# A decoder trunk on one core: modulation loads in three buffers of their own, one more buffer for output weights, row sums made one at a time

## The chip, the cores and the metric

The kernel runs on one core of one Trainium2 chip, as one launch. The metric is the device time of the launch in microseconds (us). Engines are named as in the profile: PE (TensorE, matrix products), DVE (VectorE), ACT (ScalarE), POOL (GpSimd) and SP (SyncE). SP computes nothing: it issues transfers, each in its turn, and POOL issues others.

## The reference

```python
for l in range(DEPTH):                                    # 2 layers
    mod = (silu(c) @ w_ada[l] + b_ada[l]).reshape(B, 9, 1024)
    sh1, sc1, gt1, sh2, sc2, gt2, sh3, sc3, gt3 = ...
    hn = rms_norm(h, g_ffn1[l]) * (1.0 + sc1) + sh1
    h = h + 0.5 * (1.0 + gt1) * swiglu(hn, w_ffn1_in[l], w_ffn1_out[l])
    hn = rms_norm(h, g_mix[l]) * (1.0 + sc2) + sh2
    mixed = concat([attention, rwkv7, short_conv](hn @ w_mix_in[l])) @ w_mix_out[l]
    h = h + (1.0 + gt2) * mixed
    hn = rms_norm(h, g_ffn2[l]) * (1.0 + sc3) + sh3
    h = h + 0.5 * (1.0 + gt3) * swiglu(hn, w_ffn2_in[l], w_ffn2_out[l])
# swiglu(x): gate, up = split(x @ w_in);  (silu(gate) * up) @ w_out,  width 2816
```

The sequence has 512 rows, the model 1024 channels, all in float32. The "modulation" is `mod`: 9 vectors of 1024 numbers a layer, each a product of silu(c) with a 1024 x 1024 matrix.

## The kernel before, in words

The state h is held transposed, in 8 tiles of 128 channels x 512 rows. A float32 product is made of three matmuls (`mm3`, L87 to L89): each factor is split into a high part (ACT casts it, L92, tiles wH, actH, hnH, comH) and a low part (DVE subtracts, L93, tiles wL, actL, hnL, comL), and high x high, high x low and low x high are added in PSUM. So each weight tile that lands from HBM in a raw buffer (`wraw`, two of them, `load_w` L219 and `raw` L288) costs an ACT cast and a DVE subtraction before PE can take it, and the raw buffer is free again when DVE has made wL.

Each layer is ffn1, mix, ffn2. An `ffn` (L263) has 22 columns of 128 hidden units, taken as 11 pairs p:

- The first pairs (four in layer 0's ffn1, two elsewhere) are ordinary products: a projector tile for gate and one for up per column, 24 matmuls of 128 x 512 each, then SiLU and product (L390 to L393).
- Meanwhile `combine(k)`, k = 0 to 3, makes sums and differences of the normed rows (two x, four parts of q, then the split comH and comL, L307 to L315) that the other pairs need. The scratch q lies in a buffer "first" or "crep" by turns.
- The other pairs go through `pair_in` (L332), a Strassen scheme of seven products of 24 matmuls of 128 x 256. Their weights are sums of weight blocks. S is loaded by SP (tag "chain", two buffers), and a second block is added to it by an accumulating transfer that POOL issues (`plus`, L293). Then come a11 (tag "first"), a12 (`wraw`), S3 (tag "third", load and accumulate again), and the last block (`wraw`). ACT copies PSUM results out in between (L342, L346, L351).
- The pairs are cut in two groups, g = 0 with columns 0 to 11 and g = 1 with 12 to 21. After each group comes its output product: for each of 8 output tiles i, two pieces of w_out (`pieces`, L375) and 36 or 30 matmuls, then `residual` (L258) adds to h. Between the groups' output tiles stand modulation steps.

A modulation step (`ada_steps`, L157) loads 512 KB on POOL (L164, tile `wada`) and makes one multiply with a sum on DVE (L149) with `crep`, silu(c) in all partitions. Its loads share the buffers "first", "third" and "chain" with the pairs, and `ada_crep` (L151) loads crep through SP and puts SiLU on ACT. In layer 0's ffn1 it does so twice, since combine uses its buffer in between.

A scheduler lists the instructions by the program's order and priorities, and each engine and each issuing queue then goes through its own list strictly in turn. `tc.issue_after` holds an instruction back in that list behind a named one.

The prediction uses letters for places of the span: A, the first Strassen pair of layer 0's ffn1; B, the end of that ffn's output; C, the start of layer 0's ffn2; D and F, the starts of layer 1's ffn1 and ffn2; E, the end of layer 1's ffn1; G, the start of group 1 in layer 0's ffn1.

Of the kernel before, what the change touches and what calls it, by code (L numbers as in the profile page):

```python
# [8 lines left out]
F32 = mybir.dt.float32  # L9
# [6 lines left out]
P = 128  # L16
D = 1024
T = 512
L = 2
KD = D // P  # L20
# [36 lines left out]
def trunk_kernel(ctx, tc, ins, out, layers=L, phases=("ffn1", "mix", "ffn2")):  # L57
    nc = tc.nc
# [4 lines left out]
    wp = ctx.enter_context(tc.tile_pool(name="wp", bufs=3))  # L63
# [87 lines left out]
    def ada_crep(pool):  # L151
        c = pool.tile([P, D], F32, name="crep", tag="crep", bufs=1)
        nc.sync.dma_start(c, ins["crep"])
        act(c, c, AF.Silu)
        return c

    def ada_steps(pool, crep, n, behind=None):  # L157

        with tc.issue_after(behind.ins) if behind else nullcontext():
            for m, (l, i, k) in enumerate(todo[:n]):  # L160
                if (l, i) not in mod:
                    mod[l, i] = const.tile([P, KD], F32, name=f"mod{l}_{i}")
                w = pool.tile([P, D], F32, name="wada", tag=("first", "third", "chain")[m % 3], bufs=1 + m % 3 // 2)
                nc.gpsimd.dma_start(w, ins["wadaT"][l, i, k])  # L164
                ada_dot(mod[l, i][:, k : k + 1], w, crep)
                k0 = k if m == 0 or k == 0 else k0
# [49 lines left out]
        return hn, scale, stats, apply  # L216


    def load_w(src, n=KD):  # L219

        w = wp.tile([P, KD, P], F32, name="wraw", tag="wraw", bufs=2)
        wH = wp.tile([P, KD, P], F32R, name="wH", tag="wH", bufs=4)
        wL = wp.tile([P, KD, P], F32R, name="wL", tag="wL", bufs=4)
        nc.sync.dma_start(w[:, :n], src)
        split(wH[:, :n], wL[:, :n], w[:, :n])
        return wH, wL

# [35 lines left out]
    def ffn(l, w_in, w_pair, w_out, hn, im, ss, need, then, first=None):  # L263
# [6 lines left out]
        with tc.tile_pool(name="act", bufs=1) as ap_:  # L270
# [5 lines left out]
            xs, waiting, done = {}, [], [None]  # L276

            def flush():
                for f in waiting:
                    done[0] = f()  # L280
                waiting.clear()
# [3 lines left out]
                split(*pair, w)  # L285
                return pair

            def raw(src, tag=None, bufs=1):  # L288
                w = (ap_.tile if tag else wp.tile)([P, KD, P], F32, name=tag or "wraw", tag=tag or "wraw", bufs=bufs if tag else 2)
                nc.sync.dma_start(w, src)  # L290
                return w

            def plus(w, src):  # L293
# [9 lines left out]
            def combine(k):  # L303

                x1, x2 = E("x1"), E("x2")
                for x, kk in ((x1, k), (x2, k + 4)):
                    tt(x, hn[kk][0].bitcast(F32), hn[kk][1].bitcast(F32), ALU.add)  # L307
                tag = ("first", "crep")[k % 2]
                q = ap_.tile([P, 4, H2], F32, name="q", tag=tag, bufs=1)
                tt(q[:, 0], x1[:, lo_], x1[:, hi_], ALU.subtract)  # L310
                stt(q[:, 1], x2[:, hi_], -1.0, q[:, 0], ALU.mult, ALU.subtract)
                tt(q[:, 2], x2[:, hi_], x1[:, hi_], ALU.subtract)
                stt(q[:, 3], q[:, 1], -1.0, x2[:, lo_], ALU.mult, ALU.subtract)
                split(*com[k], q)
# [17 lines left out]
            def pair_in(p):  # L332
                A = lambda g, kh: w_pair[l, p, g, kh]
                turns = ("r0", "r1") if p % 2 else ("r1", "r0")
                pD, pF, pG = (psum([P, 2, H2], n, t) for n, t in zip(("ps_d", "ps_f", "ps_g"), ("mm",) + turns))
                X = new_x(p)
                half_ = lambda n: E(n).rearrange("p (i t) -> p i t", i=2)
                S = raw(A(1, 0), "chain", 2)
                plus(S, A(1, 1))
                prod(pF, hl(S), P1, True)  # L340
                up = half_("up")
                nc.scalar.copy(up, pF)  # L342
                a11 = raw(A(0, 0), "first")
# [24 lines left out]
                def rest():  # L368
                    prod(pD, hl(raw(A(1, 1))), T4, False)
                    tt(gate, pD, gate, ALU.mult)  # L370
                    return put(X, lo_, gate)

                waiting.append(rest)

            def pieces(i, j0, j1):  # L375
                n = (j1 - j0) // 2
                for k0 in (j0, j0 + n):
                    yield k0, n, load_w(w_out[l, i, :, k0 : k0 + n], n)

            crep = None  # L380
            if n_first == 4:
                crep = ada_crep(ap_)
            for g, (j0, j1) in enumerate(GROUPS):
                for p in range(j0 // 2, j1 // 2):
                    if p < n_first:
                        X = new_x(p)
                        for j in (2 * p, 2 * p + 1):
                            pg, pu = next(tiles), next(tiles)
                            s = E("silu")
                            act(s, pg, AF.Silu)  # L390
                            stt(s, s, -1.0, pu, ALU.mult, ALU.mult)
# [12 lines left out]
                flush()  # L404
                if todo and not crep:
                    crep = ada_crep(ap_)
# [788 lines left out]
```

## Time and profile before

| | before |
|---|---|
| median of 3 runs | 2047.09 us (2045.33 to 2048.42) |
| the profiled execution | 2047.34 us |
| its span | 2045.6 us |
| mean granted clock of PE | 0.978 |
| PE busy | 1944.5 us |
| DVE busy | 1427.8 us |
| ACT busy | 840.9 us |
| POOL busy | 131.0 us |

The page gives busy time, share of the span and count of instructions. A row of a timeline has the start in the span, the time, the engine, the line, the operation, the tile written and the tiles read; in brackets stand the idle time of the engine ahead of the instruction and what ended it. In the list of waits, a row has who waited for whom, the total in us, how often, and the longest. The granted clock is 1 at full speed; rows of windows have PE's busy time in a stretch and the clock's mean in it.

### The profile page before, as it was taken

How to read it: one execution, taken by the hardware profiler on the slowest of the kernel's cores; microseconds unless marked ns; L12 is line 12 of the kernel's file. 1: busy time of each engine (PE TensorE's matmuls, PEld its weight loads, DVE VectorE, ACT ScalarE, POOL GpSimd, SP SyncE). 2: the span in 40 equal slices, each digit the busy share in tenths (PEclk: the TensorE clock that was granted, in tenths of full speed). 3: DMA queues.
4: the chain of work that ended last, by engine and by line, in shares of the span. 5: the costliest groups of instructions: out<-in, count | busy, mean ns of one | idle time of the engine just before them, and what ended most of it. 6: DMA issues, size and time to landing. Idle time of an engine off the chain costs nothing.

```text
span 2045.6 us, 32890 instructions
## 1 busy us (share of the span) xinstructions
PE 1944.5 (95%) x13428; PEld 1698.5 (83%) x13428; DVE 1427.8 (70%) x2228; ACT 840.9 (41%) x1267; POOL 131.0 (6%) x212
## 2 busy tenths in 40 slices
PE   8969999899999899999988999998999988999999
PEld 7859899786677789899877989987767767998997
DVE  6667687667875777767776776777587667673772
ACT  4433254346322345245244523533553234542551
POOL 0011111100000000110100011110000000010100
PEclk9989999999999899999988999999999998999999
DMA  7566875520122345885654577653202142564643
GB/s 285 199 178 206 274 189 167 193 75 32 53 66 89 83 151 169 278 216 171 204 150 132 171 254 236 186 189 123 83 21 76 51 134 74 164 191 119 188 114 99
DMA packets 104454, 308.72 MB, mean 151 GB/s; under 512 B 23408, under 2 KB 24432, under 8 KB 103280
## 3 DMA queue, kind: packets, MB, share of 16 engines
q1 hardware_dynamic: 76080, 203.86, 29.1%
q0 software_dynamic: 28224, 102.77, 19.6%
q8 instruction: 105, 1.72, 0.3%
q14 instruction: 45, 0.37, 0.1%
HBM read 303.18 MB, written 3.41 MB: 150 GB/s over the span
## 4 chain that ended last, share of the span: by engine, by line
PE 74%; DVE 14%; DMA 6%; ACT 4%; issue 2%; POOL 0%; ACTq 0%; SPq 0%; DVEq 0%; POOLq 0%
PE ps_mm L87 11%; PE ps_mm L88 11%; PE ps_mm L89 11%; PE ps_d L324 6%; PE ps_d L326 6%; PE ps_d L325 6%; PE ps_f L326 3%; PE ps_f L324 3%; PE ps_f L325 3%; DVE wL L93 3%; DMA wraw<-in_w1o 2%; DVE wada L149 2%; PE ps_g L324 2%; PE ps_g L326 2%; PE ps_g L325 2%
## 5 line engine op out<-in xcount | busy, mean ns | idle before, releaser
L92 ACT CAST wH<-wraw 128x1024 fp32r<-128x1024 f32 (+2 forms) x292 | 268.4, 921 | 598.1 <-PE ps_mm L88 193.0
L93 DVE TENSOR_TENSOR wL<-wraw,wH 128x1024 fp32r<-128x1024 f32 (+2 forms) x292 | 308.2, 1058 | 124.4 <-ACT wH L92 122.8
L87 PE MATMUL ps_mm<-hnH,wH 128*128 128x512 f32 (+1 forms) x760 | 281.9, 377 | 36.8 <-ACT hnH L213 30.0
L89 PE MATMUL ps_mm<-hnH,wL 128*128 128x512 f32 (+1 forms) x760 | 282.3, 373 | 17.5 <-DVE wL L93 17.5
L89 PE MATMUL ps_mm<-actH,wL 128*128 128x512 f32 (+1 forms) x744 | 283.6, 381 | 8.6 <-DVE wL L93 8.6
L88 PE MATMUL ps_mm<-hnL,wH 128*128 128x512 f32 (+1 forms) x760 | 285.3, 376 | 0.1
L87 PE MATMUL ps_mm<-actH,wH 128*128 128x512 f32 (+1 forms) x744 | 283.8, 381 | 0.5 <-ACT wH L92 0.3
L88 PE MATMUL ps_mm<-actL,wH 128*128 128x512 f32 (+1 forms) x744 | 283.1, 380 | 0.0
L324 PE MATMUL ps_d<-comH,wH 128*128 128x256 f32 x816 | 227.7, 279 | 0.1
L325 PE MATMUL ps_d<-comL,wH 128*128 128x256 f32 x816 | 225.7, 277 | 0.0
L326 PE MATMUL ps_d<-comH,wL 128*128 128x256 f32 x816 | 225.5, 276 | 0.0
L87 PEld LDWEIGHTS ps_mm<-hnH,wH 128*128 128x128 f32 x760 | 149.1, 199 | 62.9 <-ACT hnH L213 31.4
L93 DVE TENSOR_TENSOR wL<-chain,wH 128x1024 fp32r<-128x1024 f32 x102 | 124.9, 1225 | 108.7 <-ACT wH L92 108.7
L89 PEld LDWEIGHTS ps_mm<-hnH,wL 128*128 128x128 f32 x760 | 151.6, 200 | 45.5 <-DVE wL L93 20.6
L92 ACT CAST wH<-chain 128x1024 fp32r<-128x1024 f32 x102 | 107.3, 1052 | 185.3 <-PE ps_d L325 56.4
L88 PEld LDWEIGHTS ps_mm<-hnL,wH 128*128 128x128 f32 x760 | 151.6, 199 | 26.1 <-issue 4.2
L89 PEld LDWEIGHTS ps_mm<-actH,wL 128*128 128x128 f32 x744 | 142.1, 191 | 35.9 <-DVE wL L93 10.0
L149 DVE SCALAR_TENSOR_TENSOR wada<-wada,crep 128x1024 f32<-128x1024 f32 x140 | 166.2, 1219 | 7.0 <-DMA wada<-in_wadaT 6.7
L87 PEld LDWEIGHTS ps_mm<-actH,wH 128*128 128x128 f32 x744 | 142.2, 191 | 26.6 <-ACT wH L92 0.9
L88 PEld LDWEIGHTS ps_mm<-actL,wH 128*128 128x128 f32 x744 | 142.1, 191 | 25.8
L324 PEld LDWEIGHTS ps_d<-comH,wH 128*128 128x128 f32 x816 | 153.4, 188 | 3.3 <-ACT s L351 1.7
L325 PEld LDWEIGHTS ps_d<-comL,wH 128*128 128x128 f32 x816 | 153.4, 188 | 0.0
(349 smaller groups left out, 4007.3 us busy)
## 6 DMA issues: line engine op xcount, KB each, us to landing
wada<-in_wadaT POOLq DMA_DIRECT2D x128, 512.0 KB, 4.5
wraw<-in_wmi SPq DMA_DIRECT2D x40, 512.0 KB
wraw<-in_w2p SPq DMA_DIRECT2D x36, 512.0 KB
wraw<-in_w1p SPq DMA_DIRECT2D x32, 512.0 KB
wraw<-in_w1o SPq DMA_DIRECT2D x32, 384.0 KB
wraw<-in_w2o SPq DMA_DIRECT2D x32, 384.0 KB
wraw<-in_w1i SPq DMA_DIRECT2D x20, 512.0 KB
wraw<-in_w1o SPq DMA_DIRECT2D x32, 320.0 KB
```

What stands on the lines that cost most here:

```text
L87: mm(acc, wH, xH, start=start, stop=False)
L88: mm(acc, wH, xL, start=False, stop=False)
L89: mm(acc, wL, xH, start=False, stop=stop)
L92: nc.scalar.copy(hi, src)
L93: nc.vector.tensor_sub(lo, src, hi.bitcast(F32))
L149: stt(w, w, 1.0, crep, ALU.mult, ALU.mult, accum_out=out_)
L324: mm(pt[:, i], wH, x[k][0], start=start and i + k == 0, stop=False, skip_group_check=True)
L325: mm(pt[:, i], wH, x[k][1], start=False, stop=False, skip_group_check=True)
L326: mm(pt[:, i], wL, x[k][0], start=False, stop=k == 3, skip_group_check=True)
```

## The change

- Modulation's three loads go to "first", "third" and "sum1", one buffer each. The former "chain" pair of buffers becomes "sum0" and "sum1", taken by pairs of even and odd p; modulation never uses "sum0".
- q alternates between "first" and "third", not "crep": so crep is loaded once in layer 0's ffn1. Elsewhere its load is put behind the last weight load issued so far.
- `combine(k)` is called at four different tiles (`when`), not two at a time behind one column.
- Modulation steps are spread differently: in layer 0's ffn1 4, 4 and 3 behind columns 2, 3 and 6 (before 3, 3, 3 and 3), then 3 per output tile in g = 0 with two more at i = 7 in "sum1" and "third", and 2 per tile in g = 1 (before 3 at the first two tiles, then 2).
- Every third piece of w_out is loaded into "sum0" instead of one of the two `wraw` buffers, except for i = 7 in g = 0 and for the last pieces.
- The loads of the first two Strassen pairs in g = 0 are put behind the last weight load but one (`after`).

The core of the diff:

```diff
-    def ada_steps(pool, crep, n, behind=None):
+    def ada_steps(pool, crep, n, behind=None, tags=("first", "third", "sum1")):
-                w = pool.tile([P, D], F32, name="wada", tag=("first", "third", "chain")[m % 3], bufs=1 + m % 3 // 2)
+                w = pool.tile([P, D], F32, name="wada", tag=tags[m % 3], bufs=1)
...
-    def load_w(src, n=KD):
+    loads = []
+
+    def load_w(src, n=KD, raw=None):
-        w = wp.tile([P, KD, P], F32, name="wraw", tag="wraw", bufs=2)
+        w = raw or wp.tile([P, KD, P], F32, name="wraw", tag="wraw", bufs=2)
-        nc.sync.dma_start(w[:, :n], src)
+        loads.append(nc.sync.dma_start(w[:, :n], src))
...
-            def raw(src, tag=None, bufs=1):
+            def raw(src, tag=None):
-                nc.sync.dma_start(w, src)
+                with tc.issue_after(after[0].ins) if after[0] else nullcontext():
+                    nc.sync.dma_start(w, src)
...
-                tag = ("first", "crep")[k % 2]
+                tag = ("first", "third")[k % 2]
...
-                S = raw(A(1, 0), "chain", 2)
+                S = raw(A(1, 0), ("sum0", "sum1")[p % 2])
...
-            def pieces(i, j0, j1):
+            turn_ = [0]
+            def pieces(i, j0, j1, spare=False):
                 n = (j1 - j0) // 2
                 for k0 in (j0, j0 + n):
-                    yield k0, n, load_w(w_out[l, i, :, k0 : k0 + n], n)
+                    turn_[0] += spare
+                    w = ap_.tile([P, KD, P], F32, name="wraw", tag="sum0", bufs=1) if spare and turn_[0] % 3 == 0 else None
+                    yield k0, n, load_w(w_out[l, i, :, k0 : k0 + n], n, w)
...
+            when = {1: 0, 3: 1, 4: 2, 5: 3} if n_first == 2 else {8: 0, 9: 1, 10: 2, 11: 3}
...
-                            pg, pu = next(tiles), next(tiles)
+                            pg = next(tiles)
+                            if 2 * j in when:
+                                combine(when[2 * j])
+                            pu = next(tiles)
...
-                            if p == n_first - 2:
-                                for k in range(2 * (j % 2), 2 * (j % 2) + 2):
-                                    combine(k)
-                            elif p == n_first - 3:
-                                ada_steps(ap_, crep, 3, behind)
-                            elif p == n_first - 1 and n_first == 4:
-                                crep = crep if j % 2 else ada_crep(ap_)
-                                ada_steps(ap_, crep, 3, behind)
+                            if 2 * j + 1 in when:
+                                combine(when[2 * j + 1])
+                            if n_first == 4:
+                                ada_steps(ap_, crep, (0, 0, 4, 4, 0, 0, 3, 0)[j], behind)
                     else:
+                        after[0] = None if g or p > n_first + 1 else loads[-2]
                         pair_in(p)
+                        after[0] = None
                 flush()
                 if todo and not crep:
-                    crep = ada_crep(ap_)
+                    with tc.issue_after(loads[-1].ins):
+                        crep = ada_crep(ap_)
...
-                    ada_steps(ap_, crep, 0 if i == 7 else 2 if g and i > 1 else 3, done[0])
+                    if i < 7:
+                        ada_steps(ap_, crep, 2 if g else 3, done[0])
+                    elif n_first == 4:
+                        ada_steps(ap_, crep, 2, done[0], ("sum1", "third"))
...
-                    for k0_, n, w in pieces(i, j0, j1):
+                    for k0_, n, w in pieces(i, j0, j1, g or i < 7):
```

What this does to the engines' lists is shown at three places. First SP at place A, the loads between the projector weights (in_w1i) and the Strassen weights (in_w1p) of layer 0's ffn1. Before:

```order
20 L224 DMA wraw<-in_w1i 128x1024 x10
21 L290 DMA wraw<-in_w1p 128x1024 x2
22 L153 DMA crep<-in_crep 128x1024
23 L290 DMA chain<-in_w1p 128x1024
24 L290 DMA first<-in_w1p 128x1024
25 L290 DMA third<-in_w1p 128x1024
26 L290 DMA chain<-in_w1p 128x1024
```

And now:

```order
20 L226 DMA wraw<-in_w1i 128x1024 x9
21 L293 DMA sum_1006<-in_w1p 128x1024
22 L226 DMA wraw<-in_w1i 128x1024
23 L293 DMA wraw<-in_w1p 128x1024 x2
24 L293 DMA first<-in_w1p 128x1024
25 L293 DMA third<-in_w1p 128x1024
26 L293 DMA sum_1206<-in_w1p 128x1024
```

The second crep load is gone, and S of the first pair (sum_1006, in sum0) has moved ahead of the last projector weight and of two loads into wraw.

Second, DVE at place C, from the last row sum that is begun ahead of the first SiLU product (silu) on; x and q are the sums' scratch, comL the low part of a finished sum, wL that of a weight. Before:

```order
720 L391 SCALAR_TENSOR_TENSOR silu<-silu,ps_mm 128x512
721 L313 SCALAR_TENSOR_TENSOR q<-q,x_6455 128x256
722 L307 TENSOR_TENSOR x_6465<-hnH,hnL 128x512
723 L393 TENSOR_TENSOR actL<-silu,actH 128x512
724 L307 TENSOR_TENSOR x_6466<-hnH,hnL 128x512
725 L93 TENSOR_TENSOR comL<-q,comH 128x1024
726 L310 TENSOR_TENSOR q<-x_6465 128x256
727 L312 TENSOR_TENSOR q<-x_6466,x_6465 128x256
728 L311 SCALAR_TENSOR_TENSOR q<-x_6466,q 128x256
729 L93 TENSOR_TENSOR wL<-wraw,wH 128x1024
```

And now:

```order
721 L401 SCALAR_TENSOR_TENSOR silu<-silu,ps_mm 128x512
722 L316 SCALAR_TENSOR_TENSOR q<-q,x_6445 128x256
723 L93 TENSOR_TENSOR wL<-wraw,wH 128x1024
724 L403 TENSOR_TENSOR actL<-silu,actH 128x512
725 L93 TENSOR_TENSOR comL<-q,comH 128x1024
726 L310 TENSOR_TENSOR x_6491<-hnH,hnL 128x512
727 L310 TENSOR_TENSOR x_6492<-hnH,hnL 128x512
```

The weight split (wL) stood behind the rest of one sum and most of the next; now it stands directly behind the SiLU product and the last part of q.

Third, POOL from the output of group 0 to the start of group 1 in layer 0's ffn1 (place G). Before:

```order
12 L164 DMA wada<-in_wadaT 128x1024 x20
13 L294 DMA chain<-in_w1p 128x1024
14 L294 DMA third<-in_w1p 128x1024
15 L294 DMA chain<-in_w1p 128x1024
16 L294 DMA third<-in_w1p 128x1024
```

And now:

```order
12 L164 DMA wada<-in_wadaT 128x1024 x18
13 L297 DMA sum_1956<-in_w1p 128x1024
14 L164 DMA wada<-in_wadaT 128x1024 x5
15 L297 DMA sum_2156<-in_w1p 128x1024
16 L297 DMA third<-in_w1p 128x1024 x2
```

Five modulation loads, the two new ones among them, now stand between the accumulates of S for the first pair and for the second, and S3 of the first pair ("third") comes behind both of these.

More of the change, by code (lines that the diff above doesn't have):

```diff
@@ L275, in ffn @@
             tiles = (t for t in projector([w_in[l, j, g] for j in range(2 * n_first) for g in range(2)], hn, BANKS[:3], first, 1) if t is not None)
-            xs, waiting, done = {}, [], [None]
+            xs, waiting, done, after = {}, [], [None], [None]
             def flush():
@@ L286, in hl @@
                 return pair
-            def raw(src, tag=None, bufs=1):
-                w = (ap_.tile if tag else wp.tile)([P, KD, P], F32, name=tag or "wraw", tag=tag or "wraw", bufs=bufs if tag else 2)
-                nc.sync.dma_start(w, src)
+            def raw(src, tag=None):
+                w = (ap_.tile if tag else wp.tile)([P, KD, P], F32, name=tag or "wraw", tag=tag or "wraw", bufs=1 if tag else 2)
+                with tc.issue_after(after[0].ins) if after[0] else nullcontext():
+                    nc.sync.dma_start(w, src)
                 return w
@@ L373, in pair_in @@
                 waiting.append(rest)
-            def pieces(i, j0, j1):
+            turn_ = [0]
+            def pieces(i, j0, j1, spare=False):
                 n = (j1 - j0) // 2
                 for k0 in (j0, j0 + n):
-                    yield k0, n, load_w(w_out[l, i, :, k0 : k0 + n], n)
-            crep = None
-            if n_first == 4:
-                crep = ada_crep(ap_)
+                    turn_[0] += spare
+                    w = ap_.tile([P, KD, P], F32, name="wraw", tag="sum0", bufs=1) if spare and turn_[0] % 3 == 0 else None
+                    yield k0, n, load_w(w_out[l, i, :, k0 : k0 + n], n, w)
+            when = {1: 0, 3: 1, 4: 2, 5: 3} if n_first == 2 else {8: 0, 9: 1, 10: 2, 11: 3}
+            crep = ada_crep(ap_) if n_first == 4 else None
             for g, (j0, j1) in enumerate(GROUPS):
@@ L393, in ffn @@
                             behind = tt(xs[j][1], s, xs[j][0].bitcast(F32), ALU.subtract)
-                            if p == n_first - 2:
-                                for k in range(2 * (j % 2), 2 * (j % 2) + 2):
-                                    combine(k)
-                            elif p == n_first - 3:
-                                ada_steps(ap_, crep, 3, behind)
-                            elif p == n_first - 1 and n_first == 4:
-                                crep = crep if j % 2 else ada_crep(ap_)
-                                ada_steps(ap_, crep, 3, behind)
+                            if 2 * j + 1 in when:
+                                combine(when[2 * j + 1])
+                            if n_first == 4:
+                                ada_steps(ap_, crep, (0, 0, 4, 4, 0, 0, 3, 0)[j], behind)
                     else:
+                        after[0] = None if g or p > n_first + 1 else loads[-2]
                         pair_in(p)
+                        after[0] = None
                 flush()
                 if todo and not crep:
-                    crep = ada_crep(ap_)
+                    with tc.issue_after(loads[-1].ins):
+                        crep = ada_crep(ap_)
                 if g == 0:
```

## The prediction

> **What bounds the kernel now.** I read the page's busy shares, then what PE waited for in the whole span, then the granted clock around each wait, and last the timelines of the engines that PE waits for.
>
> ```profile
> PE 1944.5 (95%) x13428; PEld 1698.5 (83%) x13428; DVE 1427.8 (70%) x2228; ACT 840.9 (41%) x1267; POOL 131.0 (6%) x212
> PE 74%; DVE 14%; DMA 6%; ACT 4%; issue 2%; POOL 0%; ACTq 0%; SPq 0%; DVEq 0%; POOLq 0%
> ```
>
> PE is the bound: busy for 1944.5 of 2045.6 us. The change neither removes nor adds a matmul. So it can win only PE's idle time of about 101 us, and the time in which PE runs at a lower clock. The waits that end PE's idle time:
>
> ```profile
> PE ps_mm L87 <- ACT hnH L213: 30.0, 7, 7.2
> PE ps_mm L89 <- DVE wL L93: 26.1, 11, 4.3
> PE ps_f L324 <- ACT wH L92: 16.5, 1, 16.5
> ...
> L89 PE MATMUL ps_mm<-hnH,wL 128*128 128x512 f32 (+1 forms) x760 | 282.3, 373 | 17.5 <-DVE wL L93 17.5
> L89 PE MATMUL ps_mm<-actH,wL 128*128 128x512 f32 (+1 forms) x744 | 283.6, 381 | 8.6 <-DVE wL L93 8.6
> ```
>
> The first three rows are total, number of waits, longest. The 30.0 us on hnH are the norms between stages, which the change leaves alone. The other two belong to places that it touches. 16.5 us is a single wait for the first weight sum S of the Strassen pairs in layer 0's ffn1 (A). The 26.1 us on wL, the low part of a split weight, fall into two groups in the page: 17.5 us in the projector tiles at the start of three ffns (layer 0's ffn2, layer 1's ffn1 and ffn2: C, D, F) and 8.6 us in the output stage of three ffns (layer 0's ffn1 and ffn2, layer 1's ffn1: B, the end of ffn2, E).
>
> Behind most of these waits the granted clock falls to half (columns: window, its length, PE busy, clock, DMA share, GB/s):
>
> ```profile
> 137.90:141.80 3.90, 3.44 (x15) 0.51 0.80 144
> 397.70:401.10 3.40, 3.40 (x17) 0.50 0.66 218
> 722.20:725.60 3.40, 3.07 (x8) 0.53 0.86 278
> 1036.00:1039.40 3.40, 3.40 (x18) 0.50 0.82 271
> 1077.00:1080.40 3.40, 3.40 (x10) 0.50 0.44 154
> 1087.20:1094.00 6.80, 6.07 (x14) 0.50 0.91 286
> 1401.20:1404.60 3.40, 3.40 (x18) 0.51 0.70 229
> 1725.50:1732.30 6.80, 6.20 (x15) 0.50 0.89 297
> ```
>
> PE's work there, 32.4 us in all, would take half as long at full clock: 16.2 us. The most that the change can win is therefore 16.5 + 17.5 + 8.6 + 16.2 = 58.8 us.
>
> **The change part by part. S of the first pair and the second load of crep (A).** What stands on SP, POOL, ACT and PE there:
>
> ```profile
> 85.98 14.29 SPq L224 DMA_DIRECT2D wraw<-in_w1i  x3
> ...
> 112.01 0.33 SPq L153 DMA_DIRECT2D crep<-in_crep  x1
> 122.57 0.33 SPq L290 DMA_DIRECT2D chain<-in_w1p  x1
> ...
> 128.56 0.89 POOL L294 DMA_DIRECT2D chain<-in_w1p  x1 [6.34 <-DMA chain<-in_w1p]
> ...
> 116.81 1.06 ACT L154 ACTIVATE crep<-crep 128x1024 f32<-128x1024 f32 x1 [5.59 <-DMA crep<-in_crep]
> 136.69 1.04 ACT L92 CAST wH<-chain 128x1024 fp32r<-128x1024 f32 x1 [12.62 <-DMA chain<-in_w1p]
> ...
> 119.81 0.39 PE L87 MATMUL ps_mm<-hnH,wH 128*128 128x512 f32 x1
> ...
> 120.95 0.39 PE L89 MATMUL ps_mm<-hnH,wL 128*128 128x512 f32 x1
> 137.79 0.58 PE L324 MATMUL ps_f<-comH,wH 128*128 128x256 f32 x1 [16.45 <-ACT wH L92]
> ```
>
> S was loaded at 122.57, when modulation had given up a "chain" buffer, added to by POOL at 128.56, and cast at 136.69: 14.1 us from load to cast, begun after PE had run dry at 121. In the changed kernel S goes into sum0, which modulation never uses, and SP issues it before the last projector weight. The last three of those were issued from 85.98 on and the last of them by 100.3, so S would be cast by about 100 + 14 = 114, 7 us before PE asks for it. I remove all 16.5 us and half of 3.44, 1.7 us, of clock. The crep reload goes too; its 5.59 us on ACT are off PE's path, since the tiles went on until 121.
>
> What is late next there is S3, the sum in "third" for the pair's later product. "third" now carries modulation and the sum of row group 3 up to the last tiles; its load starts only behind them, and its accumulate stands on POOL behind the last modulation loads. How long such a sum takes is shown by the start of group 1 in the same ffn, and by all 34 of them:
>
> ```profile
> 231.99 0.33 SPq L290 DMA_DIRECT2D third<-in_w1p  x1
> ...
> 241.01 0.87 POOL L294 DMA_DIRECT2D third<-in_w1p  x1 [8.96 <-DMA third<-in_w1p]
> ...
> 248.00 1.05 ACT L92 CAST wH<-third 128x1024 fp32r<-128x1024 f32 x1 [1.88 <-PE ps_f L325]
> ...
> L92 ACT CAST wH<-third x34: 1047/1050/1056, 143.6 to 1970.3; 128x1024 fp32r<-128x1024 f32 x34
> DMA to landing us min/median/max: 5.3/6.5/8.6
> ```
>
> Load 9.0 us, accumulate 6.5 (5.3 to 8.6). The first third cast, at 143.6, came 5.8 us after the pair's first matmul at 137.79; on ACT it stands ahead of the copies that PE's next product needs. Now the pair starts near 121.2, so S3 should be there by about 127 to 128. I put the last modulation product that frees "third" at 116; with a load of 4.5 us (what modulation's equal loads take, below) and an accumulate of 6.5 to 8.6 it lands at 127 to 129.5, and later by up to 4.5 if the load is as slow as the one above. I take 3 us of wait (0 to 7), and 1.7 us of low clock behind it.
>
> **Sums one by one (C, D, F).** At C, DVE does this:
>
> ```profile
> 706.33 0.69 DVE L391 SCALAR_TENSOR_TENSOR silu<-silu,ps_mm 128x512 f32<-128x512 f32 x1 [3.55 <-ACT silu L390]
> ...
> 719.79 1.22 DVE L93 TENSOR_TENSOR comL<-q,comH 128x1024 fp32r<-128x1024 f32 x1
> ...
> 721.26 2.35 DVE L93 TENSOR_TENSOR wL<-wraw,wH 128x1024 fp32r<-128x1024 f32 x2
> ...
> 722.53 0.80 PE L89 MATMUL ps_mm<-hnH,wL 128*128 128x512 f32 x1 [4.30 <-DVE wL L93]
> ```
>
> Both weight splits at 721.26 stand behind the sums, and PE waits 4.30 us. In the changed order, shown with the change above, one sum lies between two splits. One sum is two additions of 0.68, four parts of 0.42 and a comL of 1.22: 4.3 us, and with a split (1.22) and the silu work (0.69 + 0.68) 6.8 us. A pair of tiles is 2 x 24 matmuls at 0.228 us (1.14 us for five steps from 119.81 to 120.95) = 10.9 us. So DVE no longer falls behind. Putting the new order on these durations, the splits come 1 to 4 us ahead of PE at C and D and 0.5 us ahead at F, where I count a small loss. I remove 17.5 us and 1.5 + 4.7 + 3.1 = 9.3 us of clock. Given back is S3 again: "third" is free only after the fourth sum. The load and accumulate then take 4.5 + 6.5 = 11 us. I take 0.8 us at C (0 to 1.5), 2 at D (0 to 3.5), and 3 + 1.7 of clock at F (0 to 6, and 1.7).
>
> **A third output buffer (B, end of ffn2, E).** On ACT near E and on PE:
>
> ```profile
> 1380.15 0.73 ACT L92 CAST wH<-wraw 128x640 fp32r<-128x640 f32 x1 [6.32 <-DMA wraw<-in_w1o]
> ...
> 1388.32 0.73 ACT L92 CAST wH<-wraw 128x640 fp32r<-128x640 f32 x1 [6.29 <-DMA wraw<-in_w1o]
> ...
> 1397.24 0.28 PE L89 MATMUL ps_mm<-actH,wL 128*128 128x256 f32 x1
> ...
> 1398.20 0.28 PE L88 MATMUL ps_mm<-actL,wH 128*128 128x256 f32 x1
> 1400.89 0.39 PE L89 MATMUL ps_mm<-actH,wL 128*128 128x256 f32 x1 [2.41 <-DVE wL L93]
> ```
>
> A column's two pieces come every 8.2 us (1380.15 to 1388.32), and ACT waits 6.3 us for the transfer. PE needs 30 matmuls x 0.228 = 6.8 us per column. So the loads lose 1.4 us a column until their lead is gone. A third buffer for every third piece lets about half as much again be under way. I remove all 8.6 us, and 3 x 1.7 = 5.1 us of clock.
>
> [...]
>
> **Modulation on its own buffers (G, E).** Two steps that stood elsewhere now stand at the end of group 0's output in layer 0's ffn1, in sum1 and third. S3 of group 1's first pair then loads behind a product there. Prices:
>
> ```profile
> L149 DVE SCALAR_TENSOR_TENSOR wada<-wada,crep x140: 1195/1218/1226, 15.0 to 1835.8; 128x1024 f32<-128x1024 f32 x140
> wada<-in_wadaT POOLq DMA_DIRECT2D x128, 512.0 KB, 4.5
> ```
>
> Before, that S3's load was issued at 231.99 and its cast was at 248.00, with 1.88 us of idle ACT ahead of it. Now I put the product at about 241.7, so the sum lands 11 us later, at about 252: 3.5 us of wait (0 to 7) and 1.7 of clock. In layer 1's ffn1 two steps are left over, both in "first", and run one after the other ahead of the last residual: between nothing and 4.5 + 1.2 less what lies beside PE; I take 1.2 us (0 to 3).
>
> **Sum.** Given back: waits 3 + 0.8 + 2 + 3 + 3.5 + 1.2 = 13.5, clock 3 x 1.7 = 5.1, together 18.6 us. At worst 7 + 1.5 + 3.5 + 6 + 7 + 3 = 28 of waits and 4 x 1.7 of clock, 34.8. Net 58.8 - 18.6 = 40.2 us. The profiled execution took 2047.34 us (span 2045.6), 0.25 above the median of the runs, 2047.09. So 2047.3 - 40.2 = 2007.1: I say 2007.
>
> **The rivals.** (1) All waits go and S3 is early enough everywhere: 2047.3 - 58.8 = 1988.5 us. For it: ACT idled 1.88 us ahead of the cast at 248.00, so there was slack. Against: "third" now has more users ahead of the first pair. Chance 0.13.
>
> (2) S3 is late at all its worst: 2047.3 - 58.8 + 34.8 = 2023 us. For it: the 8.96 us that POOL waited for one load. [...] Chance 0.17.
>
> (3) The third buffer brings nothing, because the pieces arrive late for another reason (DVE's modulation products and squares ahead of wL, or the DMA engines): the 8.6 + 5.1 us stay, 2007.1 + 13.7 = 2021. Chance 0.08.
>
> [...] Chance 0.03.
>
> (5) Slower: the serial chain of A returns in "third" at every first pair. A chain of buffer, load, accumulate and cast cost 16.5 + 1.7 = 18.2 us at A. There are five starts of pairs where "third" now has a new user (A, C, D, F, G): 5 x 18.2 = 91, and 2047.3 - 58.8 + 91 = 2079 us. It turns slower from 58.8 / 5 = 11.8 us each. Against: combination 4's split comes two tiles, 10.9 us, ahead of the pair at C, and PE has 5.8 us of products before the cast, 16.7 us for the 11 needed. Chance 0.04.
>
> **How the numbers follow.** The forecast has 0.55, the rivals 0.13, 0.17, 0.08, 0.03 and 0.04. The range goes from full gain, 1987, to 2028, a few microseconds over the worst of (2) and short of (2) and (3) together. What a measurement of this kernel can tell from no change is 0.2%, 4 us. Only (5) isn't faster by that; I give faster 0.95, same 0.01, slower 0.04.
>
> **What would show it.** Right: no wait of ps_f L324 on wH of 16 us, wL waits of projector and output near zero, the clock whole where the eight windows stood, and PE waits of 1 to 4 us on S3's casts or the copies behind them, near the first pairs. The S3 loads on SP would start after the fourth sum's comL. Wrong: wL waits still at the ends of the output stages (rival 3), a long wait at a pair's third or fourth product (rivals 2 and 5), or waits in the norms that grow from 30.0.

## The result, and the profile after

The changed kernel took 2027.55 us (median of 4 runs, 2020.85 to 2030.23) against 2047.27 us (median of 4, the three of before and one more): a ratio of 0.990 with a 95% interval of 0.9874 to 0.9925. It is faster by 1.0%, 19.7 us, half of the 40 that were forecast. Five further runs (below) gave 2029.37 us and 0.9913 (0.99 to 0.9926). The profiled execution is the fastest of its four: 2020.85 us, span 2018.8.

First the page's busy shares and what PE waited for in the whole span, to be held against the rows of before:

```profile
PE 1936.5 (96%) x13428; PEld 1693.8 (84%) x13428; DVE 1429.8 (71%) x2229; ACT 842.0 (42%) x1266; POOL 130.8 (6%) x212
...
PE ps_mm L87 <- ACT hnH L213: 20.1, 7, 4.5
PE ps_d L327 <- ACT s L349: 19.7, 5, 10.7
PE ps_mm L89 <- DVE wL L93: 10.5, 5, 3.9
PE ps_ss L202 <- DVE ss L189: 7.3, 3, 4.5
...
L89 PE MATMUL ps_mm<-hnH,wL 128*128 128x512 f32 (+1 forms) x760 | 279.7, 369 | 10.5 <-DVE wL L93 10.5
L89 PE MATMUL ps_mm<-actH,wL 128*128 128x512 f32 (+1 forms) x744 | 281.8, 379 | 0.0
```

Four things are to be seen. The single wait of 16.5 us for S is gone. The output stages wait for wL no more (0.0, before 8.6). The projector tiles still do, 10.5 us (before 17.5). And there is a new row of 19.7 us: in the first pairs one of PE's later products waits for ACT's copy of s (L349), and on ACT the cast of S3 stands in front of that copy. Unlooked for, the norms' wait on hnH fell from 30.0 to 20.1.

PE's idle time fell from 2045.6 - 1944.5 = 101.1 us to 2018.8 - 1936.5 = 82.3, by 18.8. The other 8.0 us are PE's busy time, for the same count of matmuls, and the mean granted clock goes with it (0.982, before 0.978). Half-clock stretches at the places of the change now:

```profile
133.60:137.00 3.40, 3.40 (x19) 0.50 0.77 247
242.80:256.50 13.70, 4.33 (x20) 0.50 0.57 146
720.70:724.10 3.40, 3.40 (x10) 0.50 0.80 231
1079.10:1082.50 3.40, 3.33 (x8) 0.50 0.46 155
1386.30:1400.00 13.70, 7.43 (x31) 0.50 0.31 103
1710.60:1714.00 3.40, 3.40 (x10) 0.50 0.59 204
```

Behind C, D and F (720, 1079, 1710) the half clock is still there, with 10.1 us of PE's work in it (18.7 in the rows of before). Behind A it is as before (3.40 us of work, before 3.44). At B there is none any more (the clock is 1.00 from 375 to 400); G (242) has a long stretch that it did not have, and E (1386) a longer one.

Place A, on SP, POOL, ACT and PE:

```profile
109.95 1.04 ACT L92 CAST wH<-sum 128x1024 fp32r<-128x1024 f32 x1
...
116.55 0.33 SPq L293 DMA_DIRECT2D third<-in_w1p  x1
...
122.14 0.89 POOL L297 DMA_DIRECT2D third<-in_w1p  x1 [13.58 <-DMA third<-in_w1p]
...
129.99 1.04 ACT L92 CAST wH<-third 128x1024 fp32r<-128x1024 f32 x1 [5.01 <-DMA third<-in_w1p]
...
133.00 0.39 PE L327 MATMUL ps_d<-comH,wH 128*128 128x256 f32 x1 [4.26 <-ACT s L349]
```

S is cast at 110, before PE asks for it. S3 is issued at 116.6 behind the modulation product, lands just before 130, and PE waits 4.26 us.

Place G, the start of group 1, on DVE, SP, POOL, ACT and PE:

```profile
233.26 1.22 DVE L149 SCALAR_TENSOR_TENSOR wada<-wada,crep 128x1024 f32<-128x1024 f32 x1
...
234.52 0.33 SPq L293 DMA_DIRECT2D third<-in_w1p  x1
...
239.68 0.88 POOL L297 DMA_DIRECT2D third<-in_w1p  x1 [1.50 <-DMA third<-in_w1p]
...
249.16 1.04 ACT L92 CAST wH<-third 128x1024 fp32r<-128x1024 f32 x1 [15.90 <-DMA third<-in_w1p]
...
252.17 0.58 PE L327 MATMUL ps_d<-comH,wH 128*128 128x256 f32 x1 [10.65 <-ACT s L349]
```

The load took 5.2 us and the accumulate 9.5 us until the cast; the cast comes at 249, where it came at 248 before, in a stage that now begins 13 us earlier (the pair's first matmul is at 232.19, before at 245.05). The accumulate took 9.5 us against a median of 6.5 before. Another sum stood on POOL's own queue, issued 2.4 us ahead of it, and SP issued a weight load at 239.91, right behind it. Whether the weight load or the sum ahead slowed the accumulate, or either did, no run here took apart.

Place C on ACT, DVE and PE:

```profile
709.55 1.05 ACT L92 CAST wH<-wraw 128x1024 fp32r<-128x1024 f32 x1 [2.54 <-DMA wraw<-in_w2i]
711.84 1.05 ACT L92 CAST wH<-sum 128x1024 fp32r<-128x1024 f32 x1 [1.24 <-DMA sum<-in_w2p]
714.46 1.06 ACT L154 ACTIVATE crep<-crep 128x1024 f32<-128x1024 f32 x1 [1.57 <-DMA crep<-in_crep]
715.43 1.03 ACT L92 CAST comH<-q 128x1024 fp32r<-128x1024 f32 x1
...
716.49 1.22 DVE L93 TENSOR_TENSOR comL<-q,comH 128x1024 fp32r<-128x1024 f32 x1 [4.61 <-ACT comH L92]
718.57 1.22 DVE L93 TENSOR_TENSOR wL<-wraw,wH 128x1024 fp32r<-128x1024 f32 x1
...
719.84 0.50 PE L89 MATMUL ps_mm<-hnH,wL 128*128 128x512 f32 x1 [2.13 <-DVE wL L93]
```

DVE isn't too busy here: it sits idle for 4.61 us. ACT's list has the casts of late arrivals (a weight, S, crep) ahead of comH, so DVE's comL waits for ACT, and the last weight's wL, whose wH was ready at 710.6, stands behind comL. At D and F the late cast in front of comH is that of S alone (ACT idles 4.28 and 2.80 us for it, and crep's SiLU comes behind comH); DVE idles 3.98 and 3.63 us there, and PE waits 3.90 and 3.72.

### The profile page after: what moved, and what is told of

Its sections match the earlier page's. It is cut to its first block, busy times and chain, and to the rows that moved or that the text cites. A ratio compares the mean times of both kernels' runs of the same rounds, so it can differ in the third digit from the quotient of the medians.

```text
span 2018.8 us, 32904 instructions
## 1 busy us (share of the span) xinstructions
PE 1936.5 (96%) x13428; PEld 1693.8 (84%) x13428; DVE 1429.8 (71%) x2229; ACT 842.0 (42%) x1266; POOL 130.8 (6%) x212
## 5 line engine op out<-in xcount | busy, mean ns | idle before, releaser
L87 PE MATMUL ps_mm<-hnH,wH 128*128 128x512 f32 (+1 forms) x760 | 279.9, 374 | 26.2 <-ACT hnH L213 20.1
L89 PE MATMUL ps_mm<-hnH,wL 128*128 128x512 f32 (+1 forms) x760 | 279.7, 369 | 10.5 <-DVE wL L93 10.5
L327 PE MATMUL ps_d<-comH,wH 128*128 128x256 f32 x816 | 229.7, 281 | 19.8 <-ACT s L349 19.7
L149 DVE SCALAR_TENSOR_TENSOR wada<-wada,crep 128x1024 f32<-128x1024 f32 x140 | 168.2, 1221 | 42.6 <-DMA wada<-in_wadaT 42.0
L93 DVE TENSOR_TENSOR wL<-sum,wH 128x1024 fp32r<-128x1024 f32 x102 | 125.0, 1225 | 72.3 <-ACT wH L92 72.3
L92 ACT CAST wH<-sum 128x1024 fp32r<-128x1024 f32 x102 | 107.3, 1052 | 152.5 <-PE ps_d L328 61.7
```

The lines of the kernel that those rows point to most:

```text
L87: mm(acc, wH, xH, start=start, stop=False)
L89: mm(acc, wL, xH, start=False, stop=stop)
L92: nc.scalar.copy(hi, src)
L93: nc.vector.tensor_sub(lo, src, hi.bitcast(F32))
L149: stt(w, w, 1.0, crep, ALU.mult, ALU.mult, accum_out=out_)
L327: mm(pt[:, i], wH, x[k][0], start=start and i + k == 0, stop=False, skip_group_check=True)
```

## The experiments

The theory from these rows: the change removes what it was forecast to remove at A, B and the output stages, but S, S3 and the weights now come from HBM in one bunch, and a late cast at the head of ACT's list, or a buffer that modulation holds, gives the time back at G, A, C, D, F and E. The rival at C, D and F is that DVE has too much work, and at G that the transfer itself is slow. All kernels but the last three are the changed kernel with one edit. Each median is of 4 to 6 runs. The kernel before was timed beside each group of kernels, with medians of 2046.72, 2046.79 and 2047.24 us, and each ratio is to the one beside it. Where a text says faster or slower than the changed kernel, the two figures are the distances to its two medians, 2029.37 and 2027.55 us.

**The changed kernel again.** 

> The changed kernel itself once more, for its spread. Its four times lie between 2020.85 and 2030.23 us, those of the kernel before between 2045.33 and 2048.42. Theory: the long waits that are left (10.7 us for S3 at G, 3.7 to 3.9 us for wL at D and F) hang on transfers that are queued closely together, so they vary from run to run; this profile then differs from the first by a few us at one or two of these places and nowhere else. Rival: the spread is one of the whole span, and every stage is longer by the same small share.

Measured: 2029.37 us (2027.22 to 2031.15). In the profile, taken at 2029.61, PE's waits are nearly the same:

```profile
PE ps_mm L87 <- ACT hnH L213: 20.0, 7, 4.5
PE ps_d L327 <- ACT s L349: 17.6, 5, 8.4
PE ps_mm L89 <- DVE wL L93: 10.2, 4, 4.4
PE ps_ss L202 <- DVE ss L189: 9.1, 3, 5.4
```

Its page has PE busy for 1946.0 of 2027.6 us, so idle for 81.6, against 82.3 in the first profile. So the 8.8 us between the two spans are all busy time. Neither theory nor rival had that: single waits differ by 2.3 us at most, and what differs is how long PE runs at half clock (mean granted clock 0.977, in the first profile 0.982). The same stretch of the mix stage, first in this profile and then in the other:

```profile
552.10:559.00 6.90, 6.90 (x32) 0.51 0.44 127
```

```profile
552.10:559.00 6.90, 6.54 (x63) 1.00 0.45 125
```

Ahead of it both have waits of 0.9 us and less. So differences of a few microseconds between kernels here are read from the waits and from medians, not from one span.

**Modulation's two steps out of G.**

```diff
-                    if i < 7:
-                        ada_steps(ap_, crep, 2 if g else 3, done[0])
-                    elif n_first == 4:
-                        ada_steps(ap_, crep, 2, done[0], ("sum1", "third"))
+                    if i < 7:
+                        ada_steps(ap_, crep, 3 if not g or (n_first == 4 and i < 2) else 2, done[0])
```

> The two modulation steps at i = 7 (sum1, third) are taken away and made in the first two output tiles of group 1 instead; nothing else changes. Theory: these steps hold the buffer third until 234.4 us, and that makes S3 of group 1's first pair late; without them the wait of 10.7 us, the 1.4 us of wL waits ahead of it and most of the low clock behind it (13.7 us at half) go: 12 to 17 us faster than the changed kernel. Rival: the accumulating transfer itself is slow there (9.5 us from its issue to the cast) because S of the second pair is loaded at the same time; then the wait shrinks by half at most: 3 to 7 us faster.

Measured: 2014.15 us (2012.52 to 2015.1), 15.2 us under the changed kernel timed beside it, ratio to before 0.9839 (0.9826 to 0.9852). The theory's 12 to 17 holds. The cast of S3 now waits for PE, not for the transfer:

```profile
232.95 1.05 ACT L92 CAST wH<-third 128x1024 fp32r<-128x1024 f32 x1 [1.88 <-PE ps_f L328]
```

The wait at G is gone altogether, and with it the half clock behind it (the clock is 1.00 from 225 to 256.5). The accumulate is now issued at 225.18, where it was at 239.68, and has landed when the cast begins at 232.95, so within 7.8 us (9.5 there).

**crep behind the pairs.**

```diff
-                    nc.sync.dma_start(w, src)
+                    last_raw[0] = nc.sync.dma_start(w, src)
...
-                    with tc.issue_after(loads[-1].ins):
+                    with tc.issue_after(last_raw[0].ins):
```

> In three ffns the load of crep and its SiLU are put behind the last Strassen pair's loads of group 0; nothing else changes. Theory: at C, D and F, DVE's comL waits for ACT, whose list has the cast of S (late from HBM) ahead of the cast comH; crep's SiLU (1.05 us) and its 512 KB are a small part: 1 to 4 us faster than the changed kernel in all. Rival: crep is what blocks ACT; then the waits of 2.1, 3.9 and 3.7 us for wL go, with their low clock: 10 to 15 us faster.

Measured: 2030.44 us (2027.6 to 2036.19), ratio 0.9924 (0.9908 to 0.9939): no gain that could be told from the changed kernel's 0.9913 (0.99 to 0.9926). So the rival falls, and the theory's small gain isn't seen either. The waits:

```profile
PE ps_d L327 <- ACT s L349: 25.6, 7, 8.6
...
PE ps_mm L89 <- DVE wL L93: 8.9, 7, 3.2
```

wL waits fell by 1 to 2 us, and the copies behind S3 cost 25.6 us in seven places instead of five. The two new waits (1.4 and 2.1 us, at 891 and 1251) stand in pairs of group 1. In the first of these two ffns crep is issued at 794.87, long before; and one such wait came with S behind the fourth weight too (2.08 us at 1238.94), which leaves crep's place in the program alone. So their cause is not shown.

**S not behind the weights.**

```diff
-                        after[0] = None if g or p > n_first + 1 else loads[-2]
+                        after[0] = None
```

> The loads of S of the first pairs are not put behind weights: SP issues them after the second projector weight, as before. Theory: S is then there long before its cast, ACT isn't blocked at C, D and F, and the wL waits (2.1, 3.9, 3.7 us) and their low clock go; but the norm before ffn2 waits for the third projector weight again (6.95 and 7.2 us as in the kernel before, against 2.1 and 2.2), with its low clock: in sum 5 us faster to 5 us slower than the changed kernel. Rival: DVE has too much to do at C, D and F whatever ACT does; then the wL waits stay and the norms' 10 us and their clock come on top: 10 to 16 us slower.

Measured: 2023.29 us (2021.43 to 2024.99), ratio 0.9884 (0.9871 to 0.9898): 4 to 6 us faster than the changed kernel, at the better end of the theory's range; the rival falls.

```profile
PE ps_mm L87 <- ACT hnH L213: 24.6, 7, 4.5
PE ps_d L327 <- ACT s L349: 22.2, 5, 10.0
...
PE ps_mm L89 <- DVE wL L93: 3.8, 3, 3.1
```

At C, D and F no wL wait is left, with the sums and DVE's work unchanged. The 3.1 us is new, in layer 0's ffn1, where the edit works too: S is now issued at 49.26, ahead of nine projector weights, and was issued at 88.34, behind them. Those weights come later: the cast that stood at 79.85 now stands at 85.09, after 8.96 us in which ACT waited for the transfer, and DVE is behind by then. And the norms' wait is only half back (24.6; 20.0 with S behind the weights, 30.0 before). That parts the 10 us gained at the norms before the two ffn2. Before, SP issued S, S3 and S again ahead of the third projector weight, at 659; S behind the weights is one half; the other goes with S3, which the sums' scratch q in "third" now holds back, though no run took that by itself apart.

**S behind the fourth weight.**

```diff
-                        after[0] = None if g or p > n_first + 1 else loads[-2]
+                        after[0] = None if g or p > n_first + 1 else loads[-2 if n_first == 4 else -5]
```

> In the three ffns that start with two pairs, the loads of S of the first Strassen pairs stand behind the fourth projector weight, not behind the seventh; ACT's list stays the same word for word. Theory: ACT isn't blocked by the cast of a late S, so the wL waits at C, D and F (2 to 4 us each, with low clock) go, and the norm keeps its short wait, since three weights and more still come first: 8 to 14 us faster than the changed kernel. Rival: what holds the third sum's comH on ACT isn't S but the slow pace of all transfers together; then the wL waits stay: within 3 us.

Measured: 2020.26 us (2010.26 to 2021.43), ratio 0.9857 (0.9836 to 0.9878): 7 to 9 us below the changed kernel's two medians, at or just under the lower end of the theory. The lists of ACT and DVE are the same word for word; what differs is when transfers are issued. At C, S goes out at 670.95 instead of 698.24, and the last projector weight and crep some 7 us later than they did. The page's row of the projector tiles, 10.5 in the changed kernel:

```profile
L89 PE MATMUL ps_mm<-hnH,wL 128*128 128x512 f32 (+1 forms) x760 | 279.3, 369 | 0.6 <-DVE wL L93 0.6
```

The 0.6 us that are left stand in the mix stages, none at C, D and F, although the last weight itself comes later. So the late S in front of comH is shown as the cause there. A part of the gain is lost again: the copies behind S3 cost 23.0 us (2.63 and 3.09 at D and F, for 1.53 and 1.52), and the norm before layer 0's ffn2 waits 3.44 us for 2.06.

**Two output buffers.**

```diff
-                    for k0_, n, w in pieces(i, j0, j1, g or i < 7):
+                    for k0_, n, w in pieces(i, j0, j1):
```

> The output's third buffer is taken away: all pieces of w_out go into the two wraw buffers again; the rest is as in the changed kernel. Theory: this buffer alone brought the 8.6 us of wL waits at B, the end of layer 0's ffn2 and E, and their low clock; without it they come back: 8 to 14 us slower than the changed kernel, 2036 to 2042 us. Rival: those waits went because modulation's dots moved (2 a tile in group 1 instead of up to 3), and the buffer brings nothing: within 3 us of the changed kernel.

Measured: 2037.65 us (2036.64 to 2039.01), ratio 0.9952 (0.9937 to 0.9966): 8 to 10 us slower. The row of the output stages is back where it was before:

```profile
L89 PE MATMUL ps_mm<-actH,wL 128*128 128x512 f32 (+1 forms) x744 | 283.9, 382 | 9.2 <-DVE wL L93 9.2
```

The theory holds: the third buffer is what removed the 8.6 us.

**Sums' scratch out of "third".**

```diff
-                tag = ("first", "third")[k % 2]
+                tag = ("first", "sum1")[k % 2]
```

> The sums' scratch q alternates between first and sum1, not first and third; so S3 of the first pair can be loaded early, and S of the second pair waits for the sums instead. Theory: the waits on S3 at A, C, D and F (4.3, 1.7, 1.5 and 1.5 us) go or halve, but S3's load and accumulate now run beside the last projector weights, and the wL waits there don't get shorter: 3 to 8 us faster than the changed kernel. Rival: S3 was late because its accumulate is slow among other transfers, not because of its buffer: the waits stay, within 2 us, or the wL waits grow by what S3 takes from the weights: up to 5 us slower.

Measured: 2022.98 us (2021.5 to 2025.47), ratio 0.9881 (0.9867 to 0.9895): 5 to 6 us faster, as the theory had it. S3's waits at C, D and F are gone, those at A and G remain, and the wL waits stay at 9.8:

```profile
PE ps_d L327 <- ACT s L349: 14.3, 3, 9.9
PE ps_mm L89 <- DVE wL L93: 9.8, 3, 4.2
```

**Two sums at once.**

```diff
-            when = {1: 0, 3: 1, 4: 2, 5: 3} if n_first == 2 else {8: 0, 9: 1, 10: 2, 11: 3}
+            when = {1: (0, 1), 3: (2, 3)} if n_first == 2 else {8: (0,), 9: (1,), 10: (2,), 11: (3,)}
...
-                                combine(when[2 * j + 1])
+                                for k in when[2 * j + 1]:
+                                    combine(k)
```

> The changed kernel with the row sums of the three ffns that start with two pairs made two at a time again, behind column 0 and behind column 1; layer 0's ffn1 stays. Theory: spreading the sums is what took the first part of the 17.5 us of wL waits; two at once put the splits behind two sums again, on top of the late S: 5 to 12 us slower than the changed kernel. Rival: the wL waits that are left come from the cast of S on ACT alone, and where the sums stand is all one: within 2 us of it.

Measured: 2031.62 us (2030.65 to 2042.11), ratio 0.9933 (0.9911 to 0.9954): 2 to 4 us slower, less than the theory's 5 to 12. The interval overlaps the changed kernel's, so by the times alone it may be no slower, and the rival isn't ruled out. The waits show more, and so do S3's load and the pair's first product at C:

```profile
PE ps_mm L89 <- DVE wL L93: 16.9, 7, 4.1
PE ps_d L327 <- ACT s L349: 13.1, 3, 8.5
...
717.59 0.33 SPq L293 DMA_DIRECT2D third<-in_w2p  x1
...
732.44 0.28 PE L327 MATMUL ps_f<-comH,wH 128*128 128x256 f32 x1
```

The wL waits are back at 16.9 us (17.5 before), so spreading the sums does remove the part that it was meant to. But S3's waits at C, D and F are gone: only A's and G's and one of 0.6 us are left. Two at a time, the fourth sum is finished a column sooner and gives "third" back sooner, and PE comes a little later: S3's load goes out 14.9 us ahead of the pair at C, where it was 5.0 us ahead (721.55 and 726.57), and 14.7 us at D, where it was 2.8. So spreading the sums, as this change does it, shortens the waits for weights and makes those for S3.

**Modulation in the first pair's buffer at A.**

```diff
-                                ada_steps(ap_, crep, (0, 0, 4, 4, 0, 0, 3, 0)[j], behind)
+                                ada_steps(ap_, crep, (0, 0, 4, 4, 0, 0, 3, 0)[j], behind, ("first", "third", "sum0"))
```

> The changed kernel, but in layer 0's ffn1 ahead of the pairs modulation uses first, third and sum0, the buffer of the first pair's S, instead of sum1. Theory: S must wait for modulation's last product again, at about 116 us, and is cast some 14 us later, 130, where PE asks at 121: a wait of 8 to 10 us for S, in which S3's wait of 4.3 us is hidden: 4 to 8 us slower than the changed kernel. Rival: the second load of crep was the whole cause of the 16.5 us, and it is gone: within 2 us.

Measured: 2035.45 us (2034.7 to 2045.03), ratio 0.9945 (0.9926 to 0.9964): 6 to 8 us slower. S is issued at 117.30 and cast at 129.35, and PE waits for it:

```profile
PE ps_f L327 <- ACT wH L92: 7.9, 1, 7.9
...
129.35 1.04 ACT L92 CAST wH<-sum 128x1024 fp32r<-128x1024 f32 x1 [5.37 <-DMA sum<-in_w1p]
```

The theory holds: S's own buffer is worth 7.9 us of wait at A. Of the rest of the 16.5 us, 5.3 go with S being issued still later before (122.57). The second crep load, which is gone, may have held modulation up by that much; no run shows that by itself, nor what makes up the last 3 us.

**Three edits at once.** The edits of G, of S behind the fourth weight and of the sums' scratch together.

> Three edits at once: modulation's two steps in group 1 instead of at i = 7, S behind the fourth weight, q in first and sum1. Theory: the three causes are separate places of the span, so the gains add up: 15 (measured for the first) + 8 to 14 + 3 to 8, so 26 to 37 us faster than the changed kernel, 1991 to 2003 us. Rival: they share the DMA engines, so that S and S3, both early, push back the weights; then at most the first edit's gain and a few us are left, 2008 to 2015 us.

Measured: 1996.99 us (1994.31 to 1998.24), ratio 0.9751 (0.9737 to 0.9765): 31 to 32 us under the changed kernel, in the theory's range and twice the rival's. One wait on S3 is left, A's:

```profile
PE ps_ss L202 <- DVE ss L189: 9.4, 3, 4.8
...
PE ps_d L327 <- ACT s L349: 4.3, 1, 4.3
```

**No steps left over (E).** As the last, and:

```diff
-                        ada_steps(ap_, crep, 3 if not g or (n_first == 4 and i < 2) else 2, done[0])
+                        ada_steps(ap_, crep, 3 if not g or i < 2 else 2, done[0])
```

> The kernel with three edits (1996.99 us) and modulation's 3 steps in the first two output tiles of group 1 in every ffn, so that no two steps are left for the end of layer 1's ffn1. Theory: the wait for ss at E (4.8 us) comes from those two steps, which stand one behind the other ahead of the last residual on DVE; it goes back to the 1.3 us of the kernel before, with some low clock: 3 to 7 us faster than that kernel. Rival: the wait is that of the squares and sums of the last tile, which are there in any case: within 1.5 us.

Measured: 1993.74 us (1992.99 to 1996.28), ratio 0.9736 (0.9719 to 0.9753), 3.3 us under the last. The two intervals overlap, so the times alone don't tell the theory from its rival; the wait does. The wait for ss at E fell from 4.8 to 1.8 us. What had held it in the changed kernel, on POOL and DVE:

```profile
1380.64 0.53 POOL L164 DMA_DIRECT2D wada<-in_wadaT  x1 [7.38 <-DVE mod L169]
...
1385.45 1.23 DVE L149 SCALAR_TENSOR_TENSOR wada<-wada,crep 128x1024 f32<-128x1024 f32 x1 [1.38 <-DMA wada<-in_wadaT]
...
1386.60 0.48 DVE L261 SCALAR_TENSOR_TENSOR h<-ps_mm,cg,h 128x256 f32<-128x256 f32 x1
```

Both left-over steps use "first", so the second load is issued only after the first product, and the last residual's first half stands behind its product.

**And S3 early at A.** As the last, and:

```diff
-                                ada_steps(ap_, crep, (0, 0, 4, 4, 0, 0, 3, 0)[j], behind)
+                                ada_steps(ap_, crep, (0, 0, 5, 4, 0, 0, 2, 0)[j], behind, ("first", "sum1") if j == 6 else ("first", "third", "sum1"))
```

> As the run before, and at A modulation has 5, 4 and 2 steps behind columns 2, 3 and 6 and leaves third alone behind column 6, so that S3 of the first pair is loaded ahead of the last projector weight. Theory: S3's wait at A (4.3 us, 1.7 us of low clock) goes: 4 to 7 us faster than the run before. Rival: the two sums loaded and accumulated together push the last projector weight back, and a wL wait of 2 to 4 us takes its place: within 2 us.

Measured: 1989.99 us (1987.79 to 1990.62), ratio 0.9712 (0.9695 to 0.9729): 3.7 us under the last, just short of the theory's 4. S3's wait at A, 3.3 us in the run before, is gone, and a wL wait of 1.16 us ahead of the last projector weight came, about half of the least that the rival named. A wait on S3 of 2.5 us in a later pair went as well, and one of 1.4 us came in another; neither was forecast. This is the fastest version: 2.9% under the kernel before. Its page has PE busy for 1932.7 of 1988.5 us:

```profile
PE 1932.7 (97%) x13428; PEld 1691.1 (85%) x13428; DVE 1427.5 (72%) x2224; ACT 842.1 (42%) x1266; POOL 130.9 (7%) x212
```

## Why the prediction was right in sign and 20 us too low

- **S at A** was right: the 16.5 us went, and S was cast at 110 (worked out: 114). S3's wait there came as forecast, 4.26 us for 3 (0 to 7), with one half-clock interval.
- **The output's third buffer** was right: 8.6 us to 0.0, and 9.2 when it is taken away.
- **Sums one by one** was mis-sized: 17.5 us were to go, 7.0 went. The step that failed is "DVE no longer falls behind". I followed DVE's list and left out ACT's: comH stands there behind the cast of S, which the same change had made late. Landing S three weights earlier takes the 10.5 us down to 0.6.
- **Modulation at G** had the right mechanism and the wrong size: 10.65 us and 1.4 us of wL waits for the 3.5 (0 to 7). I set the buffer's release, the product at 241.7 (it ended at 234.5), against a deadline on the old clock of the stage. A's gain brings PE to the product that waits behind S3's cast 11 us earlier (241.5 for 252.5), while the modulation product came only 7 us earlier than I had set it, and the accumulate took 9.5 us instead of 6.5.
- **E** had its mechanism right and its size past the bound: the wait for ss at E grew by 3.2 us, in the other profile by 4.1, for 1.2 (0 to 3).
- **The norms**, which "the change leaves alone", gained 9.9 us. S, S3 and the second S had been issued ahead of the third projector weight; I saw the move on SP and costed it at nothing.
- **S3 at C, D and F** cost 1.71, 1.53 and 1.52 us, for 0.8, 2 and 3.
- **The clock**: 16.2 us to win and 5.1 to give back, so 11.1 were forecast. PE's busy time fell by 8.0 us in one profile and, with nearly the same waits, grew by 1.5 in the other. Half-clock stretches came at G, grew at E and came back behind C, D and F. Why the two profiles differ is open.

The sum of waits was 42.6 - 13.5 = 29.1 us; measured are 18.8 in one profile and 19.5 in the other. By place it is worse: of the 42.6 us 32.1 went, and 24.3 instead of 13.5 were given back (19.7 behind S3, 1.4 on wL at G, 3.2 on ss), 7.8 us net. The norms' 9.9 us, which were not forecast, make up more than half of what was gained in waits, and that is luck. It carried the median, 2027.55, just under the range's end of 2028; the second median, 2029.37, lies past it. The sign that the prediction named for being wrong, a long wait at a pair's third or fourth product, came at G.

Of the rivals, (2), S3 at its worst, gives the nearest time (2023), but only G's wait is as bad as that. Rivals (3) and (5) are refuted. The one at 0.03, half clock that stays in the output stages, holds in part: it is gone at B, but stands at 0.51 from 1027.7 to 1037.8 at the end of layer 0's ffn2 and at 0.50 at E, now behind waits for ss and the norm and not for wL. (1), all waits gone, was not what this change does; the last kernel, at 1990, shows that its 1988 could almost be had.

## What to carry to other kernels

When a wait is removed early in a kernel, everything behind it has its deadline moved forward: work out each later buffer's release on the new time line, not on the old. Where a load is moved, follow its cast through the in-order list of the engine that makes it, and see which unrelated step stands behind it there. Buffers shared with slow background work (here modulation) should be free one full chain, load and accumulate and cast, before the next user needs them; moving such work by one stage was worth 15 us here.

## What the runs showed of the hardware

The same kernel, with PE idle for 82.3 and 81.6 us, had spans of 2018.8 and 2027.6 us: PE was busy for 9.5 us longer in the second, at a mean granted clock of 0.977 for 0.982, and ran at half clock in different places, for example from 552.1 to 559.0 in the second (0.51) and not in the first (1.00). The stretches came behind waits of different lengths: single waits of 0.9 us and less stood ahead of the one at 552, one of 2.13 us ahead of that at 720 and one of 3.90 us ahead of that at 1079 in the first profile, where PE was busy for 1.27 and 0.00 of the 3.4 us before. What sets a stretch off isn't shown here.
